# A two-layer encoder trunk: layer 0's first queries and keys as one 1024-output chunk, with the bias table and the last kept differences at other places

## The chip, the cores and the metric

The kernel runs on one core of a Trainium2 chip. The metric is the device time of one execution in microseconds (us). The engines are named as in the profile: PE is TensorE (matmuls; its weight loads are PEld), DVE is VectorE, ACT is ScalarE, POOL is GpSimd, SP is SyncE; the last three also issue DMAs.

## The reference

One sequence of 256 tokens, width 2048, passes two layers. Everything is float32.

```python
for i in range(DEPTH):                                  # 2 layers
    h = rms_norm(x, norm_attn[i])
    mkv = rms_norm(mem, norm_mem[i]) @ w_mem_kv[i]      # 256 memory tokens, 4 heads
    if i == 0:                                          # differential attention, 12 heads of 128
        q, k, v, q_m = split(h @ w_in_a, [1536, 3072, 4608])   # 5120 outputs
        q, k = rms_norm per 64 columns                  # two halves of a head
        o = (softmax(q1 k1 + bias) - lam * softmax(q2 k2 + bias)) v ; rms_norm ; * (1 - lam_init)
    else:                                               # windowed, 4 key heads, sink logit
        q, k, v, q_m = split(h @ w_in_b, [1536, 2048, 2560])
        o = softmax(q k + bias, sink) v                 # |distance| <= 128
    o_m = softmax(rms_norm(q_m) rms_norm(k_m)) v_m
    x = x + concat(o, o_m) @ w_out[i]
    x = x + square(relu(rms_norm(x, norm_mlp[i]) @ w_up[i])) @ w_down[i]   # 2048 -> 8192 -> 2048
```

The bias is one table of 32 distance buckets by 12 heads, looked up for every pair of positions.

## The kernel before, in words

**Products.** A float32 matrix is split into a high part (a cast on ACT, `split`, L450) and a low part (the difference, DVE, L451). A product of two such matrices is three matmuls: high by high, high by low, low by high (`three`, L541 to L544, or L503 to L505 in `chunk_tok`). A matmul has 128 rows of the inner dimension, 128 tokens and 512 outputs. Tokens stand as the stationary operand in two tiles t of 128.

**Weights.** All weights stream once from memory in pieces of 512 KB (128 x 1024 floats), issued on SP's queue (L395). `piece` hands out a piece whose split is done, and `fetch` keeps two more loaded and split ahead; the raw, high and low tiles are rings of four. The order of all pieces is the list `plan`.

**Seven products.** A pair is two pieces: 256 rows of the inner dimension by 1024 outputs, which with 256 tokens is a 2 x 2 by 2 x 2 block product. `seven` (L559) makes it with 7 block products, 21 matmuls, where `one_of_eight` needs 8, 24 matmuls. In exchange DVE and ACT make sums of weight blocks (`sum_pair`), differences of the token blocks (`differences`, `pair_differences`), and, once per group of outputs, sums of the side banks (`side_sums`, L578 to L581). Which pairs go so is set by tuples such as `KV_FAST` and `FAST`. `key_values` (L596) does layer 1's keys and values in this way: 8 pairs, of which 4 and 6 have seven products, four own banks (tag mm), four side banks (tag aux), and at the end own plus side (L631).

**Layer 0's input projection.** Ten chunks of 512 outputs by `chunk_tok`, 8 pieces and 96 matmuls each, in the order v0, q0, k0, v1, q1, k1, v2, q2, k2, qm (first values, first queries, first keys and so on; qm are the memory queries). During v0, `first` loads and splits x itself.

**Other work** runs between pieces. `tick` is called after each piece: it steps the light stages of all tasks that are due, and then up to `steps` heavy stages. A task has a wait and gaps, counted in ticks. Each engine then keeps the order in which its instructions were issued. Tasks that matter here:

- `prep`, the bias table: distances, then on DVE absolute values (L851), comparisons with thresholds (L852, L857), the side (L861), their sum (L863), and SP's DMA of the table to memory (L864). `PREP_AT` sets the tick, `scalars` makes lambda.
- `rows_done`, eight tasks: `bias_hot` reads 1/8 of the table back on POOL's queue (L887) and makes one-hots (L888); `bias_rows` looks the bias up with matmuls of 48 columns (L897). The heads wait for all eight.
- `norm_T`, the normalisation of queries and keys: squares on ACT (L646), their sums (L648, L649), inverse roots (L154 to L156), the product (L656, tile t2k), and the transposes on PE (L664).
- `diff_head`: the scores of a head, softmax, mix and output.

**The MLP.** The hidden state of each of 32 blocks j is made in the up projection; `keep` then makes its differences for the down projection's seven-product pairs and stores them in memory (`kept`, L1071, on ACT's queue), since the on-chip room is used by other things. The down loop runs twice (two halves of the outputs) over the 32 blocks, and `load_kept` reads a block's differences back on POOL's queue two blocks ahead. For the last four blocks `KEEP_LAST` says how many ticks after the hidden state their differences are made: for blocks 28 and 29 that falls in the down loop's first steps.

Of the kernel before, what the change touches and what calls it, by code (L numbers as in the profile page):

```python
# [32 lines left out]
BW = 14  # L33
# [3 lines left out]
KV_FAST = (4, 6)  # L37
DIFF_KV = {2: 4, 4: 6}
# [5 lines left out]
PREP_AT = 9  # L44
BGAP = 4
# [8 lines left out]
FAST = tuple(j for j in LATE if j not in (11, 20))  # L54
# [5 lines left out]
KEEP_LAST = (10, 18, 26, 34)  # L60
# [14 lines left out]
def trunk(ctx: ExitStack, tc: tile.TileContext, xin, xtok, memin, memtok, posrel, gcol, rows,  # L75
          w_a, w_b, w_kv, w_mem, w_out, w_up, w_down, out):
# [159 lines left out]
    weights = {"a": w_a, "b": w_b, "kv1": w_kv, "mem0": w_mem[0], "mem1": w_mem[1], "out0": w_out[0], "out1": w_out[1],  # L236
# [21 lines left out]
    for layer, (name, chunks) in enumerate((("a", (6, 0, 3, 7, 1, 4, 8, 2, 5, 9)), ("b", range(4)))):  # L258
        if layer:
            plan_pairs("kv1", 8, 1)  # L260
# [22 lines left out]
    def sums_tag(key):  # L283
        if key[0].startswith(("up", "kv")):
            return "h2"
# [40 lines left out]
    for i, (name, c, j) in enumerate(plan):  # L326
        at_piece.setdefault({"a": ("in", 0), "b": ("in", 1), "kv1": ("in", 1)}.get(name, (name[:-1], int(name[-1]) if name[-1].isdigit() else 0)), i)
# [27 lines left out]
    def sum_pair(name, c, p):  # L355
# [3 lines left out]
        up = name.startswith(("up", "kv"))  # L359
# [17 lines left out]
    def fetch(parts=1, lead=None):  # L377
# [18 lines left out]
        if name.startswith(("kv", "out", "up", "down")) and j % 2 == 0:  # L396
# [199 lines left out]
    def key_values(X2):  # L596
# [3 lines left out]
        for j in range(8):  # L600
            if j == KV_FAST[0]:
                side = [bank("aux") for _ in range(4)]
            if j in DIFF_KV:
                i = DIFF_KV[j]
# [7 lines left out]

            if j in KV_FAST:
                seven(own, side, j == KV_FAST[0], j == KV_FAST[-1], two, sums.pop(("kv1", 0, j)), at, diffs[j])
# [10 lines left out]
            if j == KV_FAST[-1]:  # L625
# [8 lines left out]
    def norm_T(ps, st, nseg, g, later=False):  # L634
# [35 lines left out]
        return (hi, lo), Task([Light(squares, 1), Light(rows, ROWS_GAP), tr][not later:], wait=WAIT if later else 1, gap=WAIT)  # L670
# [300 lines left out]
    def mem_ahead(j):  # L971
        if j == 5:
            load_mem(0)

    def mem_part(layer, qm, qd, H2):
        M2 = Halves()

        def before(j):
            if j % 2 == 0:
                if j:  # L980
                    mem_raw.pop(j // 2 - 1)
                if j < 6:
                    load_mem(j // 2 + 1)
            for k in (2 * j, 2 * j + 1):
                src = mem_raw[j // 2][:, k % 4, :]
                make_x2(M2, k, src, gc[:, G_MEM + layer * KT + k:G_MEM + layer * KT + k + 1])

# [64 lines left out]
    def mlp(layer, X2, last):  # L1052
# [9 lines left out]

        def keep(j, wait):
# [5 lines left out]
            def store():  # L1069
                kept[j] = dp.tile([P, 2, 512], F32R, name=nm("kept"))  # L1070
                nc.scalar.dma_start(as32(kept[j]), as32(box.pop()))  # L1071

            box = []
            Task([Light(make, KEEP_GAP), Light(store, 0)], wait=wait)
# [14 lines left out]
        def to_hidden(q, n, u, i, tag):  # L1089
# [14 lines left out]
            if any(j in fast_pairs(f"down{layer}", h) for h in range(2)):  # L1104
                keep(j, KEEP_AFTER[2 * n + i] if q < 7 else KEEP_LAST[2 * n + i])
# [46 lines left out]
        for half_ in range(2):  # L1152
# [30 lines left out]
            def load_kept(j):  # L1183
                if j in fast:
                    diff_in[j] = quad("h2", (P, 2, 512))
                    nc.gpsimd.dma_start(diff_in[j], kept[j])

            load_kept(1)
            for j in range(32):
# [6 lines left out]
                two.append(piece(f"down{layer}", half_, 2 * j + 1))  # L1196
                at = ats.popleft()
# [59 lines left out]
    rows_done = [Task([lambda i=i: bias_hot(i), lambda i=i: bias_rows(i, bias)], [prep], wait=BW, gap=BGAP) for i in range(8)]  # L1257
# [3 lines left out]
    loads = Task([lambda c=c: load_residual(c) for c in range(4)], wait=RES_AT, gap=RES_GAP, front=True)  # L1261
    for g in range(3):
# [23 lines left out]
    ps = chunk_tok("a", 9, X2, mem_ahead)  # L1286
# [20 lines left out]
    ps = chunk_tok("b", 3, X2, mem_ahead)  # L1307
# [74 lines left out]
```

## Time and profile before

| what | value |
|---|---|
| time, median of 3 runs | 2066.44 us (2066.3 to 2066.57) |
| the profiled execution's own time | 2068.06 us |
| its span, first to last instruction | 2066.3 us |
| PE, DVE, ACT busy | 2059.5, 1824.9, 1295.9 us |
| granted PE clock | 1.000 |
| v0 on PE ends, q0 begins | 28.7 us |
| kv chunk of layer 1 ends on PE | 1134.2 us |

The profile's times are from the start of the span. "PE mm L543 <- DVE lo L451: 1.3, 2, 0.8" reads: before matmuls of line 543 into a tile named mm, PE waited for the tile lo that DVE writes in line 451, 1.3 us in all, in 2 places, 0.8 us the longest. In a timeline, a row is a start, a duration, the engine, line and operation, out <- in with shapes, and in brackets the idle time before it with what ended it. Successive instructions of one engine overlap a little, so that the time that one takes from its engine is the distance of the starts.

### The profile page before, as it was taken

The page shows a single profiled execution, that of the slowest core. Times are in us where ns is not written, and L with a number is a line of the kernel's source. Part 1 is how long each engine was busy: PE and PEld are TensorE (multiplying, and loading weights), DVE is VectorE, ACT ScalarE, POOL GpSimd, SP SyncE. Part 2 cuts the span into 40 slices and gives each one's busy share as a digit, 9 for nine tenths or more (in the row PEclk, how much of TensorE's full clock was granted, in tenths as well). Part 3 has the DMA queues.
Part 4 walks back from the last instruction along what each step waited for, and adds up shares of the span by engine and source line. Part 5 has one row for each costly group of instructions (what it writes and reads, how often), then busy time and mean ns, then how long its engine had stood idle before and what let it go on. Part 6 is the DMA issues. An engine that isn't in the chain of part 4 may idle for free.

```text
span 2066.3 us, 28900 instructions
## 1 busy us (share of the span) xinstructions
PE 2059.5 (100%) x9966; PEld 1711.5 (83%) x9966; DVE 1824.9 (88%) x2659; ACT 1295.9 (63%) x1933; POOL 190.5 (9%) x292
## 2 busy tenths in 40 slices
PE   9999999999999999999999999999999999999999
PEld 7888888888888888888888888888888888888887
DVE  7677787898998999999999778889999999999998
ACT  7467665556566576767756556556566566676764
POOL 1200111100011100000002110000001111000000
PEclk9999999999999999999999999999999999999999
DMA  9678997877898998989978887577799999898994
GB/s 318 242 240 269 279 290 227 276 232 245 277 292 285 308 322 300 389 282 322 365 295 274 262 251 262 174 234 244 246 296 298 311 306 349 309 379 308 329 374 144
DMA packets 176099, 589.08 MB, mean 285 GB/s; under 512 B 20464, under 2 KB 21488, under 8 KB 174576
## 3 DMA queue, kind: packets, MB, share of 16 engines
q1 hardware_dynamic: 134128, 439.36, 59.5%
q0 software_dynamic: 36208, 127.94, 23.7%
q10 hardware_dynamic: 5616, 19.93, 2.4%
q8 instruction: 78, 1.28, 0.2%
q14 instruction: 69, 0.57, 0.1%
HBM read 552.42 MB, written 108.13 MB: 320 GB/s over the span
## 4 chain that ended last, share of the span: by engine, by line
PE 94%; DVE 3%; DMA 2%; issue 1%; ACT 1%; SPq 0%; DVEq 0%; ACTq 0%
PE mm L543 12%; PE mm L544 12%; PE mm L542 12%; PE aux L544 11%; PE aux L542 11%; PE aux L543 11%; PE mm L503 6%; PE mm L504 6%; PE mm L505 6%; DVE lo L451 1%; PE aux L687 1%; PE mm L1097 1%; PE aux L664 1%; PE aux L1097 1%; DMA kept<-h 1%
## 5 line engine op out<-in xcount | busy, mean ns | idle before, releaser
L451 DVE TENSOR_TENSOR lo<-raw,hi 128x1024 fp32r<-128x1024 f32 (+1 forms) x492 | 583.5, 1205 | 116.6 <-ACT hi L450 115.7
L450 ACT CAST hi<-raw 128x1024 fp32r<-128x1024 f32 (+1 forms) x492 | 495.6, 1035 | 287.8 <-PE mm L505 95.7
L503 PE MATMUL mm<-hi,x 128*128 128x512 f32 x576 | 231.5, 404 | 0.1
L504 PE MATMUL mm<-lo,x 128*128 128x512 f32 x576 | 225.6, 392 | 0.2 <-DVE lo L451 0.2
L505 PE MATMUL mm<-hi,x 128*128 128x512 f32 x576 | 225.2, 391 | 0.0
L450 ACT CAST h<-big 128x1024 fp32r<-128x1024 f32 (+1 forms) x100 | 100.4, 1021 | 131.7 <-DVE big L291 84.3
L542 PE MATMUL mm<-hi,x 128*128 128x512 f32 x464 | 181.3, 391 | 0.0
L543 PE MATMUL mm<-lo,x 128*128 128x512 f32 x464 | 180.7, 389 | 0.0
L544 PE MATMUL mm<-hi,x 128*128 128x512 f32 x464 | 180.6, 389 | 0.0
L543 PE MATMUL mm<-lo,h 128*128 128x512 f32 (+1 forms) x448 | 174.2, 389 | 1.3 <-DVE lo L451 1.3
L542 PE MATMUL mm<-hi,h 128*128 128x512 f32 (+1 forms) x448 | 174.1, 389 | 0.0
L544 PE MATMUL mm<-hi,h 128*128 128x512 f32 (+1 forms) x448 | 173.7, 388 | 0.0
L450 ACT CAST hi<-big 128x1024 fp32r<-128x1024 f32 (+1 forms) x138 | 120.8, 902 | 77.1 <-PE aux L544 35.9
L542 PE MATMUL aux<-hi,x 128*128 128x512 f32 x400 | 156.3, 391 | 0.0
L544 PE MATMUL aux<-hi,x 128*128 128x512 f32 x400 | 155.7, 389 | 0.0
L543 PE MATMUL aux<-lo,x 128*128 128x512 f32 x400 | 155.7, 389 | 0.0
L542 PE MATMUL aux<-hi,h 128*128 128x512 f32 x392 | 152.8, 390 | 0.0
L544 PE MATMUL aux<-hi,h 128*128 128x512 f32 x392 | 152.5, 389 | 0.0
L543 PE MATMUL aux<-lo,h 128*128 128x512 f32 x392 | 152.5, 389 | 0.0
L451 DVE TENSOR_TENSOR lo<-big,hi 128x1024 fp32r<-128x1024 f32 (+1 forms) x138 | 139.6, 1032 | 6.8 <-ACT hi L450 6.4
L451 DVE TENSOR_TENSOR h<-big,h 128x1024 fp32r<-128x1024 f32 (+1 forms) x100 | 116.8, 1179 | 30.8 <-ACT h L450 30.0
L505 PEld LDWEIGHTS mm<-hi,x 128*128 128x128 f32 x576 | 108.1, 188 | 23.8 <-DVE x L447 0.2
(318 smaller groups left out, 4452.5 us busy)
## 6 DMA issues: line engine op xcount, KB each, us to landing
raw<-in_w_up SPq DMA_DIRECT2D x164, 512.0 KB, 6.5
madesum<-in_w_down POOLq DMA_DIRECT2D x140, 512.0 KB, 6.6
raw<-in_w_down SPq DMA_DIRECT2D x112, 512.0 KB, 6.5
big<-in_w_up SPq DMA_DIRECT2D x92, 512.0 KB, 5.0
raw<-in_w_a SPq DMA_DIRECT2D x72, 512.0 KB, 5.3
h<-kept POOLq DMA_DIRECT2D x72, 512.0 KB, 6.9
raw<-in_w_out SPq DMA_DIRECT2D x52, 512.0 KB, 5.3
big<-in_w_down SPq DMA_DIRECT2D x46, 512.0 KB, 5.7
```

The lines of the kernel that those rows point to most:

```text
L450: nc.scalar.copy(hi, src)
L451: return nc.vector.tensor_tensor(lo, src, as32(hi), op=ALU.subtract)
L503: nc.tensor.matmul(ps[t], lhsT=xh, rhs=hi[:, ws], start=(k == 0), stop=False)
L504: nc.tensor.matmul(ps[t], lhsT=xh, rhs=lo[:, ws], start=False, stop=False)
L505: nc.tensor.matmul(ps[t], lhsT=xl, rhs=hi[:, ws], start=False, stop=(k == KT - 1))
L542: nc.tensor.matmul(acc_, lhsT=x(0), rhs=w2[0][:, ws], start=first_, stop=False)
L543: nc.tensor.matmul(acc_, lhsT=x(0), rhs=w2[1][:, ws], start=False, stop=False)
L544: nc.tensor.matmul(acc_, lhsT=x(1), rhs=w2[0][:, ws], start=False, stop=last_)
L664: nc.tensor.transpose(out=pt[:, h * P:(h + 1) * P], in_=qn[t][:, h * P:(h + 1) * P], identity=ident)
L687: nc.tensor.transpose(out=pt[:, kt * S + qt * P:kt * S + (qt + 1) * P], in_=p_of(qt)[:, kt * P:(kt + 1) * P], identity=ident)
L1097: nc.tensor.transpose(out=pt[:, oo * S + t * P:oo * S + (t + 1) * P], in_=u[n][t][:, o * P:(o + 1) * P], identity=ident)
```

## The change

1. q0 and k0 become one chunk of 1024 outputs, weights `w_qk` in pair layout, run by `two_chunks("qk0")`, which is `key_values` with a name; pairs 4 and 6 have seven products. `w_a` keeps the other eight chunks.
2. The bias table's tasks come later: `PREP_AT` 9 becomes 20, the hot rows' wait `BW` 14 becomes 22 and their gap 4 becomes 2, each of the eight tasks following the one three before it. `scalars` moves ahead. Two heavy steps for each tick are in v1 where they were in q0.
3. Blocks 28 and 29 of the hidden state no longer go through `keep`: in the first half of the down loop their differences are made in place two blocks ahead (`make_kept`), and stored then for the second half. Of the list of late blocks, 26 is left out of the seven-product pairs where 20 was.
4. The first memory rows are loaded one piece earlier, and the first pair of them is split in the chunk before; the layer-1 keys' norm has a rows gap of 2.

```diff
-BW = 14
+BW = 22
-KV_FAST = (4, 6)
-DIFF_KV = {2: 4, 4: 6}
+A_CHUNKS = (4, 5, 0, 2, 6, 1, 3, 7)
+TWO_FAST = (4, 6)
+DIFF_TWO = {2: 4, 4: 6}
-PREP_AT = 9
-BGAP = 4
+PREP_AT = 20
+BGAP = 2
-FAST = tuple(j for j in LATE if j not in (11, 20))
+FAST = tuple(j for j in LATE if j not in (11, 26))
-KEEP_LAST = (10, 18, 26, 34)
+KEEP_LATE = (28, 29)
...
+        if layer == 0:
+            plan_chunks(name, chunks[:1])
+            plan_pairs("qk0", 8, 1)
+            chunks = chunks[1:]
+        else:
             plan_pairs("kv1", 8, 1)
...
-    def key_values(X2):
+    def two_chunks(name, X2):
...
-            two = [piece("kv1", 0, 2 * j + i) for i in range(2)]
+            two = [piece(name, 0, 2 * j + i) for i in range(2)]
...
+        def store_kept(j, t2):
+            kept[j] = dp.tile([P, 2, 512], F32R, name=nm("kept"))
+            nc.scalar.dma_start(as32(kept[j]), as32(t2))
...
-                keep(j, KEEP_AFTER[2 * n + i] if q < 7 else KEEP_LAST[2 * n + i])
+                if j not in KEEP_LATE:
+                    keep(j, KEEP_AFTER[2 * n + i])
...
             def load_kept(j):
-                if j in fast:
+                if j in fast and (half_ or j not in KEEP_LATE):
                     diff_in[j] = quad("h2", (P, 2, 512))
                     nc.gpsimd.dma_start(diff_in[j], kept[j])
+
+            def make_kept(j):
+                if half_ == 0 and j in KEEP_LATE:
+                    diff_in[j] = quad("h2", (P, 2, 512))
+                    differences(diff_in[j], hids[j])
+                    Task([Light(lambda t2=diff_in[j]: store_kept(j, t2), 0)], wait=KEEP_GAP)
...
-    prep = Task([Light(load_rows, 0), Light(bias_distance, 0), Light(bias_float, PREP_AT - ROWS_AT)]
-                + [Light(f, 1) for f in (bias_size, scalars, lambda: bias_steps(12, 16), lambda: bias_steps(23, 32),
+    prep = Task([Light(load_rows, 0), Light(bias_distance, 0), Light(bias_float, 3), Light(scalars, PREP_AT - ROWS_AT - 3)]
+                + [Light(f, 1) for f in (bias_size, lambda: bias_steps(12, 16), lambda: bias_steps(23, 32),
...
-        ps = chunk_tok("a", 6 + g, X2, lead=first if g == 0 else None)
-        steps = 2 if g == 0 else 1
+        ps = chunk_tok("a", next(a_chunks), X2, lead=first if g == 0 else None, steps=2 if g == 1 else 1)
...
+            ps, ks = two_chunks("qk0", X2)
         else:
             val_f32(v, ps, st0)
-        ps = chunk_tok("a", g, X2, steps=steps)
+            ps = chunk_tok("a", next(a_chunks), X2)
         qT, qd = norm_T(ps, st0, 8, gs[:, 0:1])
-        ps = chunk_tok("a", 3 + g, X2)
-        kT, kd = norm_T(ps, st0, 8, gc[:, G_AK:G_AK + 1])
+        if g:
+            ks = chunk_tok("a", next(a_chunks), X2)
+        kT, kd = norm_T(ks, st0, 8, gc[:, G_AK:G_AK + 1])
...
-    kT, kd = norm_T(kv[0], st1, 4, gc[:, G_BK:G_BK + 1])
+    kT, kd = norm_T(kv[0], st1, 4, gc[:, G_BK:G_BK + 1], rows_gap=2)
```

In the changed kernel all lines stand some 5 (in the down loop some 20) further on: L451 is L456, L503 to L505 are L508 to L510, L543 is L548, L631 is L636, L648 and L649 are L653 and L654, L656 is L661, L664 is L669, L851 to L863 are L856 to L868, L1071 is L1084.

**How instructions move.** VectorE, around the bias table. In the kernel before, at the end of v0 and the start of q0 (lo are low parts of pieces, t2k_394, t2k_395 and t2k_310 the table's tiles):

```order
L451 TENSOR_TENSOR lo_314<-raw_312,hi_313 128x512
L852 TENSOR_SCALAR t2k_395<-t2k_394 128x512
L861 TENSOR_SCALAR t2k_310<-t2k_310 128x512
L857 SCALAR_TENSOR_TENSOR t2k_395<-t2k_394,t2k_395 128x512
L451 TENSOR_TENSOR lo_329<-raw_327,hi_328 128x1024
L857 SCALAR_TENSOR_TENSOR t2k_395<-t2k_394,t2k_395 128x512
L451 TENSOR_TENSOR lo_335<-raw_333,hi_334 128x1024
L857 SCALAR_TENSOR_TENSOR t2k_395<-t2k_394,t2k_395 128x512 x3
L451 TENSOR_TENSOR lo_359<-raw_357,hi_358 128x1024
L857 SCALAR_TENSOR_TENSOR t2k_395<-t2k_394,t2k_395 128x512 x2
```

In the changed kernel, from the first side sum (row 78 of VectorE's order) on; lo_713 and lo_719 are the low parts of v1's first two pieces, aux_573 to aux_575 side banks of the new stage, mm_355 to mm_358 its own banks:

```order
L583 TENSOR_TENSOR t2k_696<-aux_574,t2k_695 128x512
L456 TENSOR_TENSOR lo_713<-raw_711,hi_712 128x1024
L584 TENSOR_TENSOR t2k_698<-aux_573,t2k_696 128x512
L585 TENSOR_TENSOR t2k_697<-t2k_696,aux_575 128x512
L456 TENSOR_TENSOR lo_719<-raw_717,hi_718 128x1024
L586 TENSOR_TENSOR t2k_699<-t2k_697,aux_573 128x512
L856 SCALAR_TENSOR_TENSOR t2k_705<-t2k_310 128x512
L636 TENSOR_TENSOR t2k_695<-mm_355,t2k_695 128x512
L857 TENSOR_SCALAR t2k_706<-t2k_705 128x512
L636 TENSOR_TENSOR t2k_698<-mm_356,t2k_698 128x512
L862 SCALAR_TENSOR_TENSOR t2k_706<-t2k_705,t2k_706 128x512
L636 TENSOR_TENSOR t2k_697<-mm_357,t2k_697 128x512
```

and further on, up to v1's third piece (lo_782, row 102) and the table's end (L868):

```order
L862 SCALAR_TENSOR_TENSOR t2k_706<-t2k_705,t2k_706 128x512
L654 TENSOR_SCALAR sm_758<-sm_758,st_102 128x8
L862 SCALAR_TENSOR_TENSOR t2k_706<-t2k_705,t2k_706 128x512
L653 TENSOR_REDUCE sm_769<-t2k_770 128x8
L456 TENSOR_TENSOR lo_782<-raw_780,hi_781 128x1024
L654 TENSOR_SCALAR sm_769<-sm_769,st_102 128x8
L653 TENSOR_REDUCE sm_769<-t2k_774 128x8
L866 TENSOR_SCALAR t2k_310<-t2k_310 128x512
L654 TENSOR_SCALAR sm_769<-sm_769,st_102 128x8
L868 TENSOR_TENSOR t1k_799<-t2k_706,t2k_310 128x512
```

The table's operations, which stood one to three at a time between low parts at 25 to 36 us, now stand between the side sums, the own sums and the norm's sums, all of them ahead of lo_782 but the last two.

PE, at the first transposes of the queries. In the kernel before (tiles t2k_625 and t2k_627 are the normalised q0; hi_1083 and hi_1107 are v1's fourth and fifth pieces):

```order
L503 MATMUL mm_1045<-hi_1083,x_195 128x512
L504 MATMUL mm_1045<-lo_1084,x_195 128x512
L505 MATMUL mm_1045<-hi_1083,x_195 128x512
L664 MATMUL aux_1148<-ident,t2k_625 128x128 x4
L664 MATMUL aux_1155<-ident,t2k_627 128x128 x4
L503 MATMUL mm_1044<-hi_1107,x_223 128x512
```

In the changed kernel (hi_781 is v1's third piece, hi_827 its fourth; t2k_810 and t2k_812 the normalised q0):

```order
L508 MATMUL mm_779<-hi_781,x_168 128x512
L509 MATMUL mm_779<-lo_782,x_168 128x512
L510 MATMUL mm_779<-hi_781,x_168 128x512
L508 MATMUL mm_778<-hi_827,x_195 128x512
L509 MATMUL mm_778<-lo_828,x_195 128x512
L510 MATMUL mm_778<-hi_827,x_195 128x512
L508 MATMUL mm_779<-hi_827,x_195 128x512
L669 MATMUL aux_894<-ident,t2k_810 128x128 x4
L509 MATMUL mm_779<-lo_828,x_195 128x512
L669 MATMUL aux_901<-ident,t2k_812 128x128 x4
```

The transposes stood behind v1's fourth piece, with k0's whole chunk, and bias rows, between them and the end of q0. They stand now within v1's fourth piece, some 40 matmuls behind the end of the chunk that holds q0.

ACT, at the start of layer 0's down projection, before (h_8130 holds block 28's differences):

```order
L450 CAST h_8130<-t2k_8131 128x512
L450 CAST h_8155<-blk_5517 128x512
L450 CAST hi_8137<-big_4688 128x1024
L450 CAST hi_8160<-t2k_7999 128x512
L1071 DMA kept_8188<-h_8130 128x1024
L450 CAST h_8204<-blk_5891 128x512
L450 CAST x_8147<-blk_7818 128x1024
```

In the changed kernel, 100 rows later, in the 27th step of the loop:

```order
L455 CAST x_9158<-blk_7872 128x1024
L455 CAST h_9119<-t2k_9120 128x512
L1084 DMA kept_9150<-h_9119 128x1024
L455 CAST hi_9061<-raw_9060 128x1024
L455 CAST hi_9076<-raw_9075 128x1024
```

The store of block 28's differences, and the cast that makes them, moved from the first steps of the loop to its 27th.

More of the change, by code (lines that the diff above doesn't have):

```diff
@@ L256, in plan_pairs @@
         plan.extend((name, h, j) for h in range(halves) for j in range(2 * n))
-    for layer, (name, chunks) in enumerate((("a", (6, 0, 3, 7, 1, 4, 8, 2, 5, 9)), ("b", range(4)))):
-        if layer:
+    for layer, (name, chunks) in enumerate((("a", A_CHUNKS), ("b", range(4)))):
+        if layer == 0:
[3 more added lines that the diff above has]
+        else:
             plan_pairs("kv1", 8, 1)
@@ L283, in sums_tag @@
     def sums_tag(key):
-        if key[0].startswith(("up", "kv")):
+        if key[0].startswith(("up", "qk", "kv")):
             return "h2"
@@ L395, in fetch @@
             behind[0] = nc.sync.dma_start(raw, src)
-        if name.startswith(("kv", "out", "up", "down")) and j % 2 == 0:
+        if name.startswith(("qk", "kv", "out", "up", "down")) and j % 2 == 0:
             if down:
@@ L611, in at @@
                 return pair[:, kk, part, t * P:(t + 1) * P]
-            if j in KV_FAST:
-                seven(own, side, j == KV_FAST[0], j == KV_FAST[-1], two, sums.pop(("kv1", 0, j)), at, diffs[j])
+            if j in TWO_FAST:
+                seven(own, side, j == TWO_FAST[0], j == TWO_FAST[-1], two, sums.pop((name, 0, j)), at, diffs[j])
             elif j < 7:
@@ L632, in key_values, with norm_T @@
         return u
[L634 removed]
+    def norm_T(ps, st, nseg, g, later=False, rows_gap=ROWS_GAP):
         dim = 512 // nseg
@@ L669, in norm_T @@
             squares()
-        return (hi, lo), Task([Light(squares, 1), Light(rows, ROWS_GAP), tr][not later:], wait=WAIT if later else 1, gap=WAIT)
+        return (hi, lo), Task([Light(squares, 1), Light(rows, rows_gap), tr][not later:], wait=WAIT if later else 1, gap=WAIT)
     def val_f32(v, ps, st):
@@ L969, in load_mem, with memory, mem_ahead, ahead @@
         nc.sync.dma_start(mem_raw[i], memin[:, 1024 * i:1024 * i + 1024].rearrange("p (k s) -> p k s", s=S))
-    def mem_ahead(j):
-        if j == 5:
-            load_mem(0)
+    mem_x2 = {}
+    def memory(layer, j):
+        if j == 0:
+            mem_x2[layer] = Halves()
+        if j % 2 == 0:
+            if j:
+                mem_raw.pop(j // 2 - 1)
+            if j < 6:
+                load_mem(j // 2 + 1)
+        for k in (2 * j, 2 * j + 1):
+            src = mem_raw[j // 2][:, k % 4, :]
+            make_x2(mem_x2[layer], k, src, gc[:, G_MEM + layer * KT + k:G_MEM + layer * KT + k + 1])
+    def mem_ahead(layer):
+        def ahead(j):
+            if j == 4:
+                load_mem(0)
+            if j == 7:
+                memory(layer, 0)
+        return ahead
     def mem_part(layer, qm, qd, H2):
-        M2 = Halves()
+        M2 = mem_x2[layer]
         def before(j):
[L979 to L986, printed above, removed]
+            if j < 7:
+                memory(layer, j + 1)
         ps = chunk_tok(f"mem{layer}", 0, M2, before)
@@ L1067, in make @@
                 differences(box[0], hidden(j))
-            def store():
-                kept[j] = dp.tile([P, 2, 512], F32R, name=nm("kept"))
-                nc.scalar.dma_start(as32(kept[j]), as32(box.pop()))
             box = []
-            Task([Light(make, KEEP_GAP), Light(store, 0)], wait=wait)
+            Task([Light(make, KEEP_GAP), Light(lambda: store_kept(j, box.pop()), 0)], wait=wait)
         def h2_of(j):
@@ L1253, in trunk @@
     bias = big([P, 12, 2, S])
-    prep = Task([Light(load_rows, 0), Light(bias_distance, 0), Light(bias_float, PREP_AT - ROWS_AT)]
-                + [Light(f, 1) for f in (bias_size, scalars, lambda: bias_steps(12, 16), lambda: bias_steps(23, 32),
+    prep = Task([Light(load_rows, 0), Light(bias_distance, 0), Light(bias_float, 3), Light(scalars, PREP_AT - ROWS_AT - 3)]
+                + [Light(f, 1) for f in (bias_size, lambda: bias_steps(12, 16), lambda: bias_steps(23, 32),
                                          lambda: bias_steps(46, 64, 91), bias_side, bias_table)], wait=ROWS_AT, gap=1)
-    rows_done = [Task([lambda i=i: bias_hot(i), lambda i=i: bias_rows(i, bias)], [prep], wait=BW, gap=BGAP) for i in range(8)]
+    rows_done = []
+    for i in range(8):
+        rows_done.append(Task([lambda i=i: bias_hot(i), lambda i=i: bias_rows(i, bias)], [prep] + rows_done[max(0, i - 3):i - 2],
+                              wait=BW, gap=BGAP))
     Task([lambda: bias_save(bias)], rows_done)
```

35 lines of the change are left out of this document (19 added, 16 removed).

## The prediction

> **What bounds the kernel now.** I read the page first, then the waits of TensorE, then the windows around each place that the change touches.
>
> ```profile
> PE 2059.5 (100%) x9966; PEld 1711.5 (83%) x9966; DVE 1824.9 (88%) x2659; ACT 1295.9 (63%) x1933; POOL 190.5 (9%) x292
> ...
> PE 94%; DVE 3%; DMA 2%; issue 1%; ACT 1%; SPq 0%; DVEq 0%; ACTq 0%
> ```
>
> The first line is busy time by engine, the second the chain that ended last. TensorE runs without a break, so a matmul more or less is worth its issue interval, and a wait of TensorE is worth its length. VectorE at 88% is the next in line: it is off the path on average, and decides wherever much of its work stands ahead of a piece's low part.
>
> ```profile
> PE mm L543 <- DVE lo L451: 1.3, 2, 0.8
> PE aux L142 <- DVE ones L139: 1.1, 1, 1.1
> PE aux L664 <- DVE t2k L656: 0.7, 1, 0.7
> PE mm L504 <- DVE lo L451: 0.2, 1, 0.2
> PE aux L687 <- DVE t2k L805: 0.2, 1, 0.2
> ```
>
> These are the waits of TensorE (total, times, longest). So there is little to gain by removing waits: 1.5 us from the first and fourth rows, which the change touches, and 0.7 us in the third. Each ends on VectorE. Now the windows (length, then busy PE, PEld, DVE, ACT, POOL; then clock, DMA share and GB/s):
>
> ```profile
> 12.00:30.00 18.00, 18.00 (x77) 14.33 (x78) 17.77 (x43) 13.38 (x26) 1.67 (x3) 1.00 1.02 358
> 30.00:48.00 18.00, 18.00 (x81) 14.79 (x80) 14.97 (x24) 14.64 (x29) 2.81 (x6) 1.00 0.94 322
> 48.00:90.00 42.00, 42.00 (x397) 34.84 (x396) 29.08 (x43) 19.09 (x26) 14.80 (x27) 1.00 0.76 273
> 780.00:810.00 30.00, 29.18 (x130) 23.81 (x129) 28.59 (x35) 20.61 (x25) 1.59 (x3) 1.00 0.87 292
> ```
>
> The first 30 us have full DMA and a nearly full VectorE; from 48 to 90 us VectorE has 13 us to spare. At 780 to 810 us, the start of layer 0's down projection, it is full again.
>
> **The seven-product pairs.** Six matmuls of 512 columns go. Their interval, from the layer-1 twin of the new stage, where 24 of them lie between two rows:
>
> ```profile
> 1134.22 0.39 PE L503 MATMUL mm<-hi,x 128*128 128x512 f32 x1
> ...
> 1139.66 0.39 PE L503 MATMUL mm<-hi,x 128*128 128x512 f32 x1
> ```
>
> (1139.66 - 1134.22) / 24 = 0.2267 us; six are **-1.4**. The price is VectorE work at the stage's end. The twin shows it:
>
> ```profile
> 1130.48 0.68 DVE L578 TENSOR_TENSOR t2k<-aux,t2k 128x512 f32<-128x512 f32 x1
> ...
> 1134.79 0.67 DVE L648 TENSOR_REDUCE sm<-t2k 128x4 f32<-128x512 f32 x1
> 1135.39 0.68 DVE L631 TENSOR_TENSOR t2k<-mm,t2k 128x512 f32<-128x512 f32 x1
> 1135.98 0.22 DVE L649 TENSOR_SCALAR sm<-sm,st 128x4 f32<-128x4 f32 x1
> 1136.11 0.68 DVE L648 TENSOR_REDUCE sm<-t2k 128x4 f32<-128x512 f32 x1
> ...
> 1138.16 1.22 DVE L451 TENSOR_TENSOR lo<-raw,hi 128x1024 fp32r<-128x1024 f32 x1
> 1139.30 0.16 DVE L154 TENSOR_TENSOR sm<-sm 128x8 f32<-128x8 f32 x1
> ```
>
> Start to start, a 128x512 operation takes 0.60 us, L649 0.13 and a low part 1.14. There the first side sum starts 3.74 us before the next chunk's first matmul (1134.22), and that chunk's third piece has its low part at 1139.3. TensorE reaches it at the chunk's 26th matmul, 1139.9: in time by half a microsecond. So the twin has no room for more.
>
> In the changed order there is more. Between the first side sum and the low part of v1's third piece (rows 78 to 101) stand, on VectorE: nine operations of the bias table, four side sums, four of L636, three reductions (L653), two L654 and two low parts. The bias operations' price:
>
> ```profile
> 25.48 0.68 DVE L851 SCALAR_TENSOR_TENSOR t2k<-t2k 128x512 f32<-128x512 f32 x1
> 26.08 0.68 DVE L451 TENSOR_TENSOR lo<-raw,hi 128x512 fp32r<-128x512 f32 x1
> 26.69 0.41 DVE L852 TENSOR_SCALAR t2k<-t2k 128x512 f32<-128x512 f32 x1
> 27.02 0.41 DVE L861 TENSOR_SCALAR t2k<-t2k 128x512 f32<-128x512 f32 x1
> 27.36 0.68 DVE L857 SCALAR_TENSOR_TENSOR t2k<-t2k,t2k 128x512 f32<-128x512 f32 x1
> 27.96 1.21 DVE L451 TENSOR_TENSOR lo<-raw,hi 128x1024 fp32r<-128x1024 f32 x1
> ```
>
> That is 0.60 each for L851 and L857, 0.33 for L852. So 19 operations of 0.60, one of 0.33, two of 0.13 and two of 1.14: 14.3 us. Call E the end of the new stage on TensorE. The last side bank is finished 25 matmuls earlier (row 258 of 283); with 0.3 us to pass it on, the sums start at E - 5.4, and the third low part is done at E - 5.4 + 14.3 + 1.2 = E + 10.1. TensorE needs it after 26 matmuls, E + 5.9. **+4.2**, part of it already at v1's first matmul, whose bank L636 frees late. VectorE is then late for the next two things as well. Eleven matmuls on (2.5 us) comes the fourth piece's low part, with 1.9 us of other rows and 1.2 of its own ahead: **+0.6**. Three matmuls later TensorE meets q0's transposes, which want t2k_810: small operations 0.5, a low part 1.14 and the product 0.60 against 0.7 of matmuls: **+1.6**. In the kernel before, k0's whole chunk lay between q0's end and these transposes. Bounds of the three together: 0, if the cover of 51 matmuls from the side bank sufficed, to 8.
>
> Inside the new stage ACT has a raw piece's cast, which needs a free slot of the ring of four, ahead of the cast of the first pair's sum, so that sum's parts come about 0.5 late, and the second pair's 0.15: **+0.65** (bounds 0 and 2; by the ring's place in the order only, no row shows it).
>
> **The bias rows.** The table goes to memory and comes back before TensorE can use it:
>
> ```profile
> 35.51 0.69 DVE L863 TENSOR_TENSOR t1k<-t2k,t2k 128x512 bf16<-128x512 f32 x1
> 39.35 0.43 SPq L864 DMA_DIRECT2D bkt<-t1k  x1
> 45.19 4.88 POOL L887 DMA_DIRECT2D blk<-bkt  x9 [24.33 <-DMA bkt<-t1k]
> 53.99 0.75 DVE L888 TENSOR_SCALAR blk<-blk,itf 128x2048 bf16<-128x2048 bf16 x1
> 61.58 1.38 PE L897 MATMUL aux<-tab,blk 128*128 128x48 bf16 x48
> ```
>
> From the store's issue to the first one-hot's end are 54.74 - 39.35 = 15.4 us, and TensorE came 6.8 later. In the change the table ends near E + 12 (five rows after that third low part), the one-hot at E + 27.4 by the same span, or E + 24.4 if the two transfers land in two thirds of their time, as VectorE and DMA are emptier there. TensorE is at that place, 36 rows past the transposes, at E + 24.1. **+1.4**, bounds 0.3 and 3.3. The bias rows end a chunk later, and three heads' scores then come together on four banks: **+0.4** (0 to 1.2; before, the heads' work shows only the 0.2 at L687). What moves out of 25 to 36 us frees the first chunk's change: the 0.2 at L504 goes, **-0.2**.
>
> **The kept differences.** At the down projection's start ACT's queue stands behind the store of a difference:
>
> ```profile
> 792.84 6.17 DMA kept<-h
> ...
> 799.02 0.62 ACT L450 CAST h<-blk 128x512 fp32r<-128x512 f32 x1 [2.79 <-DMA kept<-h]
> ...
> 800.63 1.22 DVE L451 TENSOR_TENSOR x<-big,x 128x1024 fp32r<-128x1024 f32 x1 [1.41 <-ACT x L450]
> ...
> 804.78 0.39 PE L542 MATMUL mm<-hi,h 128*128 128x512 f32 x1
> 805.99 0.50 PE L543 MATMUL mm<-lo,h 128*128 128x512 f32 x1 [0.82 <-DVE lo L451]
> ...
> 1767.53 5.86 DMA kept<-h
> ...
> 1780.37 0.50 PE L543 MATMUL mm<-lo,h 128*128 128x512 f32 x1 [0.50 <-DVE lo L451]
> ```
>
> A cast waits for that store's end to reuse its buffer, VectorE idles 1.41 us for the cast, TensorE is late by 1.21 - 0.23 = 0.98 us, and 0.66 in layer 1 (0.50 and the same 0.16 of restart). With these two differences moved to the loop's 27th and 28th steps the store isn't there: **-1.6** (bounds 0, if VectorE's full window makes its own lateness, and -1.9). At the new place their VectorE work, about 1.4 us each, lies in a stretch with room:
>
> ```profile
> 810.00:1085.00 275.00, 275.00 (x1222) 227.71 (x1221) 264.49 (x317) 186.63 (x239) 16.37 (x31) 1.00 0.91 329
> ```
>
> 10.5 us idle of 275, TensorE never waiting: 0, and up to +1 each if all fell in one step. The four loads that go from POOL's queue are covered by the same stretch.
>
> **The rest.** VectorE's and TensorE's orders in layer 1's key norm are the same with a rows gap of 2, so its 0.7 us stays. The memory load and first memory pair a little earlier lie in a stretch without waits: 0.
>
> **Sum**: -1.4 - 0.2 - 1.6 + 4.2 + 0.6 + 1.6 + 0.65 + 1.4 + 0.4 = +5.65. The profiled execution took 2068.06 us with a span of 2066.3; the three runs' median is 2066.44. The difference is applied to that: 2072.1, I say **2072.0**.
>
> **Rivals.** About 0.2% (4.1 us: under 2062.3 or over 2070.6) is what a measurement can tell from no change.
>
> *The sums find cover.* Everything at v1 is one race: the block of VectorE work against 51 matmuls (11.6 us). From under 10.1 us of block, instead of 14.3, TensorE waits for none of the three, and the gains stand alone: 2066.44 - 3.2 = 2063.2 with the rest at 0. For it: VectorE idles 13 us of the 42 around. Against: that idle time lies elsewhere, as the block starts with a bank that TensorE finishes late. Only with layer 1's 0.7 gone as well, and some, does it pass 2062.3. Chance 0.17, of which 0.05 below 2062.3.
>
> *Half of it.* The sums, the fourth piece and the transposes overlap more than I add (3 us in all) and the one-hot comes in time: 2066.4 to 2068. For it: each later wait is counted from the previous one's end. Chance 0.17.
>
> *A slower clock after the pause.* All windows above have clock 1.00, with no wait over 1.1 us. Here TensorE would pause 3 to 4 us in one go. If the clock then halved, the 14 matmuls up to the transposes would cost 14 x 0.227 = 3.2 us more, of which 0.6 + 1.6 are waits for VectorE anyway: +1.0, or the full 3.2 if it comes where nothing waits: 2073 to 2075. [...] Chance 0.10.
>
> *Transfers late.* The new stage loads two pairs ahead, while the windows before 48 us already show 0.94 to 1.02 of DMA. A 512 KB piece at 358 GB/s is 1.5 us; two pieces out of turn give +3: 2075. Against: the kernel before ran these windows without a wait. Chance 0.08.
>
> My forecast has the remaining 0.48. Slower by over 0.2%: 0.45 of it, the clock and the transfers, 0.63; same: 0.32; faster: 0.05. The range: 2063.5 to 2076 leaves about a tenth at either end; the forecast's own is 2070 to 2074.5.
>
> **What would show it.** In the changed profile, waits of TensorE at L509 or L508 on L456 or L636 between 70 and 85 us, some 5 us in all, and at L669 on L661 about 1.6. Right at the down projections: no store of a kept difference there, no wait at L548. Wrong: no wait over 1 us in the first 90 us; or waits on DMA there, which would be the fourth rival; or a clock below 1.00 behind the pause.

## The result and the profile after

The changed kernel takes 2079.15 us (median of 4 runs, 2078.08 to 2083.84) against 2066.37 us: a ratio of 1.0059, 95% interval 1.0047 to 1.0071, 12.8 us slower. Slower was forecast as likeliest, but 2072.0 us with a range up to 2076: the sign was right and the size was less than half of it. The profiled execution took 2079.69 us with a span of 2077.9, 11.6 over the span before.

The page of the changed kernel, busy time and the chain that ended last:

```profile
PE 2062.0 (99%) x9960; PEld 1711.8 (82%) x9960; DVE 1839.1 (89%) x2687; ACT 1299.4 (63%) x1940; POOL 189.9 (9%) x288
...
PE 88%; DVE 6%; DMA 3%; ACT 1%; issue 1%; SPq 0%; ACTq 0%; DVEq 0%
```

Six matmuls are gone, and VectorE's share of the chain has doubled. TensorE's waits (total, times, longest):

```profile
PE mm L509 <- DVE lo L456: 3.5, 2, 3.3
PE aux L669 <- DVE t2k L661: 2.2, 4, 1.2
PE aux L711 <- ACT blk L451: 1.7, 1, 1.7
PE aux L143 <- DVE ones L140: 1.1, 1, 1.1
PE aux L902 <- DVE blk L893: 1.0, 1, 1.0
PE mm L548 <- DVE lo L456: 0.7, 2, 0.5
PE mm L508 <- DVE t2k L636: 0.6, 1, 0.6
PE mm L508 <- ACT hi L455: 0.5, 1, 0.5
...
PE aux L711 <- DVE sm L717: 0.4, 1, 0.4
```

The first, fifth and seventh rows are v1 and the first bias rows, as forecast. The second is only in small part the transposes of q0: most of it lies at 290 us (1.2) and in layer 1 (0.7, as before). The third and the last are scores of heads, which were forecast at 0.4 us in all.

VectorE's timeline at the end of the new stage: the first side sum, the first operation of the bias table, the first of L636, and the low part of v1's third piece.

```profile
67.02 0.68 DVE L583 TENSOR_TENSOR t2k<-aux,t2k 128x512 f32<-128x512 f32 x1
...
71.68 0.69 DVE L856 SCALAR_TENSOR_TENSOR t2k<-t2k 128x512 f32<-128x512 f32 x1
72.28 0.69 DVE L636 TENSOR_TENSOR t2k<-mm,t2k 128x512 f32<-128x512 f32 x1
...
81.27 1.22 DVE L456 TENSOR_TENSOR lo<-raw,hi 128x1024 fp32r<-128x1024 f32 x1
```

The block is 81.27 - 67.02 = 14.25 us long; the prediction had 14.3. TensorE behind it, and the windows (busy PE, PEld, DVE, ACT, POOL, then clock, DMA share, GB/s) of its pause and of the time after:

```profile
82.54 0.79 PE L509 MATMUL mm<-lo,x 128*128 128x512 f32 x1 [3.29 <-DVE lo L456]
83.13 0.63 PE L510 MATMUL mm<-hi,x 128*128 128x512 f32 x1
83.56 0.63 PE L509 MATMUL mm<-lo,x 128*128 128x512 f32 x1
```

```profile
78.80:82.50 3.70, 0.46 (x3) 0.03 (x1) 3.70 (x8) 2.42 (x5) 0.00 (x0) 0.99 0.00 0
82.50:86.00 3.50, 3.46 (x9) 2.73 (x10) 3.50 (x11) 0.43 (x2) 0.00 (x0) 0.53 0.61 181
```

After the pause the granted clock is 0.53 and matmuls come 0.43 us apart instead of 0.227: the third rival's slow clock is there.

**Where the 11.6 us lie.** Against the interval that each kind of matmul has when nothing waits, I summed what every interval had too much, in both traces, by stretch. After minus before:

| stretch of the program | us |
|---|---|
| start and v0 | +0.2 |
| q0 and k0, v1 up to the first bias rows (28 to 100 us) | +7.8 |
| the rest of layer 0's attention (100 to 310 us) | +5.5 |
| six matmuls fewer | -1.4 |
| start of layer 0's down projection | -1.0 |
| start of layer 1's down projection | -0.8 |
| end of layer 0's down projection and layer 1's keys and values | +0.7 |
| end of layer 1's down projection | +0.5 |
| remaining stretches together | +0.1 |

The prediction's terms for the second row are 0.65 + 4.2 + 0.6 + 1.6 + 1.4 - 0.2 = 8.25. So the block at v1 was sized right. The third row had 0.4.

VectorE in that stretch, windows of the kernel before and then of the changed kernel:

```profile
100.00:141.00 41.00, 41.00 (x262) 32.96 (x261) 29.55 (x89) 25.35 (x55) 1.62 (x2) 1.00 0.65 233
...
200.00:260.00 60.00, 60.00 (x312) 49.67 (x312) 44.07 (x101) 36.88 (x81) 7.73 (x10) 1.00 0.91 279
```

```profile
100.00:141.00 41.00, 41.00 (x459) 34.04 (x458) 23.93 (x28) 18.35 (x23) 10.93 (x18) 1.00 0.69 231
...
200.00:260.00 60.00, 60.00 (x318) 49.57 (x317) 46.89 (x123) 38.09 (x92) 7.23 (x9) 1.00 0.82 244
```

From 100 to 141 us VectorE does 5.6 us less work than before, and ACT 7.0 less, because no head has begun (the first scores are at 141.72 us; before, at 112.25). That work comes later, into stretches where pieces and norms need the same engines. Of the third row some 4 us lie between 141 and 200 us and 3 between 200 and 310; up to 141 us the changed kernel loses about 1 us less than the kernel before, whose first heads are there.

### The profile page after: what moved, and what is told of

Its sections match the earlier page's. It is cut to its first block, busy times and chain, and to the rows that moved or that the text cites. A ratio compares the mean times of both kernels' runs of the same rounds, so it can differ in the third digit from the quotient of the medians.

```text
span 2077.9 us, 28913 instructions
## 1 busy us (share of the span) xinstructions
PE 2062.0 (99%) x9960; PEld 1711.8 (82%) x9960; DVE 1839.1 (89%) x2687; ACT 1299.4 (63%) x1940; POOL 189.9 (9%) x288
## 4 chain that ended last, share of the span: by engine, by line
PE 88%; DVE 6%; DMA 3%; ACT 1%; issue 1%; SPq 0%; ACTq 0%; DVEq 0%
PE mm L548 12%; PE mm L549 12%; PE mm L547 12%; PE aux L549 11%; PE aux L548 11%; PE aux L547 11%; PE mm L508 4%; PE mm L510 4%; PE mm L509 4%; DVE lo L456 2%; DMA raw<-in_w_kv 1%; PE aux L1116 1%; PE mm L1116 1%; DMA raw<-in_w_a 1%; PE aux L692 1%
## 5 line engine op out<-in xcount | busy, mean ns | idle before, releaser
L456 DVE TENSOR_TENSOR lo<-raw,hi 128x1024 fp32r<-128x1024 f32 (+1 forms) x488 | 578.6, 1206 | 124.7 <-ACT hi L455 123.7
L455 ACT CAST hi<-raw 128x1024 fp32r<-128x1024 f32 (+1 forms) x488 | 490.6, 1035 | 285.6 <-PE mm L510 81.0
L508 PE MATMUL mm<-hi,x 128*128 128x512 f32 x512 | 205.8, 403 | 1.2 <-DVE t2k L636 0.6
L510 PE MATMUL mm<-hi,x 128*128 128x512 f32 x512 | 201.5, 394 | 0.0
L548 PE MATMUL mm<-lo,x 128*128 128x512 f32 x514 | 200.6, 390 | 0.5 <-DVE lo L456 0.5
L549 PE MATMUL mm<-hi,x 128*128 128x512 f32 x514 | 200.3, 390 | 0.0
L547 PE MATMUL mm<-hi,x 128*128 128x512 f32 x514 | 199.4, 391 | 0.4 <-ACT hi L455 0.4
L548 PE MATMUL mm<-lo,h 128*128 128x512 f32 (+1 forms) x450 | 174.7, 388 | 0.2 <-DVE lo L456 0.2
L548 PE MATMUL aux<-lo,x 128*128 128x512 f32 x402 | 156.5, 389 | 0.0
L548 PE MATMUL aux<-lo,h 128*128 128x512 f32 x392 | 152.6, 389 | 0.0
L456 DVE TENSOR_TENSOR lo<-big,hi 128x1024 fp32r<-128x1024 f32 (+1 forms) x140 | 142.3, 1037 | 3.6 <-ACT hi L455 3.3
L456 DVE TENSOR_TENSOR h<-big,h 128x1024 fp32r<-128x1024 f32 (+1 forms) x100 | 116.9, 1180 | 30.1 <-ACT h L455 29.3
L509 PEld LDWEIGHTS mm<-lo,x 128*128 128x128 f32 x512 | 97.0, 189 | 22.4 <-DVE lo L456 5.1
```

The costliest lines, as they stand in the source:

```text
L455: nc.scalar.copy(hi, src)
L456: return nc.vector.tensor_tensor(lo, src, as32(hi), op=ALU.subtract)
L508: nc.tensor.matmul(ps[t], lhsT=xh, rhs=hi[:, ws], start=(k == 0), stop=False)
L509: nc.tensor.matmul(ps[t], lhsT=xh, rhs=lo[:, ws], start=False, stop=False)
L510: nc.tensor.matmul(ps[t], lhsT=xl, rhs=hi[:, ws], start=False, stop=(k == KT - 1))
L547: nc.tensor.matmul(acc_, lhsT=x(0), rhs=w2[0][:, ws], start=first_, stop=False)
```

## The experiments

The theory was that one cause, the bias table's operations put into the busy end of the new stage, makes both large rows: directly at v1, and through late heads afterwards. The rivals: the seven-product sums alone are too much; the slow clock; the other parts of the change. Times are medians; ratios are against the kernel before, run on the same chip in the same set. Its median was 2068.29 in the first set, 2067.45 and 2067.4 in the others.

### The table at its old tick

```diff
-PREP_AT = 20
+PREP_AT = 9
```

> The changed kernel with the bias table's operations back at tick 9 (PREP_AT 9 in place of 20), all else as changed. My theory: the nine bias operations (5.2 us of VectorE) between the first side sum and the low part of v1's third piece are what makes TensorE wait. Without them the block is 9.1 us instead of 14.3, and TensorE's 51 matmuls (11.6 us) cover it: the wait of 3.45 us there, the 0.8 at v1's first matmul, the 1.1 before the first bias rows and the slow clock behind the pause go, 6 to 8 us in all: 2071 to 2073. Rival: the side sums and the norm alone are too much, the wait shrinks to 1 to 2 us and stays, 2075 to 2077.

2067.96 us, ratio 1.0001 (0.9991 to 1.001). Its waits:

```profile
PE mm L548 <- DVE lo L456: 1.6, 3, 0.8
...
PE aux L711 <- DVE sm L717: 0.6, 1, 0.6
PE aux L669 <- DVE t2k L661: 0.4, 1, 0.4
PE mm L509 <- DVE lo L456: 0.2, 1, 0.2
```

With this one number the 12 us are gone, 4 to 6 more than expected. No wait is left at v1's third piece, none at the first bias rows, and from 100 to 310 us TensorE loses less than 1 us more than in the kernel before, so the heads' loss came from the table's place as well. In exchange the new stage now waits in its first half (0.8 and 0.5 us at 37 and 42 us), which makes up for the six matmuls and the kept differences.

The wait at v1 went, but not because the block shrank as expected. VectorE's first side sum and the low part of v1's third piece, then TensorE's first matmul with that low part:

```profile
68.50 0.68 DVE L583 TENSOR_TENSOR t2k<-aux,t2k 128x512 f32<-128x512 f32 x1
...
80.94 1.22 DVE L456 TENSOR_TENSOR lo<-raw,hi 128x1024 fp32r<-128x1024 f32 x1
```

```profile
82.22 0.50 PE L509 MATMUL mm<-lo,x 128*128 128x512 f32 x1
```

The block is 80.94 - 68.50 = 12.4 us long, not 9.1: the table's nine operations left it, but two one-hots (L893), two copies of looked-up bias (L903) and some more of the norm came into it. In return TensorE looks up two of the eight groups of bias rows ahead of the third piece, at 73.88 and 77.48 us, which lengthens the cover by 1.2 us each. The low part is ready at 82.16 us, just in time for 82.22. So the run shows what the table's place is worth; whether the side sums and the norm alone would fit under 51 matmuls, the rival's question, it doesn't show.

### Late heads by themselves

The kernel before, where nothing but the bias rows' start is moved:

```diff
-BW = 14
+BW = 24
```

> The kernel before with nothing changed but the bias rows ten ticks later (BW 24 instead of 14), so that the first heads' scores stand 96 matmuls (22 us) later, about where the changed kernel has them; its table, its chunks and VectorE's work around v1 are as before. Theory: late heads cost by themselves, since their VectorE and ACT work is crowded into fewer chunks; waits at scores and at the transposes of later queries appear as in the changed kernel: 3 to 4.6 us more than before. Rival: the cost of the heads in the changed kernel came from three of them in one go and the backlog that v1's wait left; here 0 to 1 us.

2073.31 us, ratio 1.0024 (1.0016 to 1.0033): 3.3 to 6.8 us slower, without any other part of the change. The profiled execution is the fastest of its eleven; its waits, and the two windows from above:

```profile
PE aux L664 <- DVE sm L714: 1.8, 1, 1.8
...
PE aux L664 <- DVE t2k L656: 0.9, 2, 0.6
PE mm L543 <- DVE lo L451: 0.8, 1, 0.8
PE mm L503 <- ACT hi L450: 0.6, 1, 0.6
PE aux L706 <- ACT x L446: 0.3, 1, 0.3
```

```profile
100.00:141.00 41.00, 41.00 (x368) 33.56 (x368) 25.87 (x53) 21.18 (x37) 1.62 (x2) 1.00 0.69 242
...
200.00:260.00 60.00, 59.73 (x326) 48.85 (x323) 46.50 (x126) 38.59 (x93) 7.24 (x9) 1.00 0.81 243
```

As in the changed kernel, VectorE has less to do up to 141 us, more after 200, and TensorE waits for transposes of a later chunk. So late heads cost by themselves, and about as much as the changed kernel loses in its third row. The places are the same only in part. Here the first scores are at 133.82 us, 21.6 us later than before, and one head follows another by 3.9 us; in this profile TensorE loses 4.7 us more than before from 200 to 310 us, and nothing more from 141 to 200. The changed kernel lost 3 us in the former stretch and 4 in the latter, with heads 29 us late and three heads' scores within 4 us. Whether those 4 us come from the greater lateness, from the three heads in one go or from the backlog behind v1 was not tried apart; the run with the table at its old tick shows that they go with the table's place.

### The pause and the clock

> The changed kernel with 14 matmuls (3.2 us) of no use put ahead of v1's third piece, where TensorE pauses 3.45 us; their result is not read. Theory: the pause makes the half clock behind it (seven intervals of 0.427 instead of 0.227), so here the clock stays 1.00 and the intervals 0.227; but VectorE sets the time of the next low part and of the transposes, so TensorE waits there instead, and the total stays within 0.5 us of the changed kernel: 2078.7 to 2079.6. Rival: the half clock costs by itself, 7 times 0.2: 2077.7.

```diff
+            if w == "a" and c == A_CHUNKS[1] and j == 2:
+                spare = bank()
+                for _ in range(FILL):
+                    nc.tensor.matmul(spare, lhsT=X2[0][:, 0, 0:P], rhs=hi[:, 0:512], start=True, stop=True)
             hi, lo = piece(w, c, j, lead and (lambda i: lead(2 * j + i)))
```

With FILL = 14: 2077.26 us, ratio 1.0047 (1.0032 to 1.0062). Five of the matmuls went into the 0.8 us wait at v1's first matmul, nine ahead of the third piece, where the wait is 1.0 us; the clock stays at 1.00. It is 1.9 us under the changed kernel's median (2.5 by the ratios, since the two were run in different sets), as the rival said, but the two intervals overlap. So this run doesn't decide what the slow clock costs.

> The changed kernel with 4 matmuls of no use ahead of v1's third piece instead of 14: the pause becomes some 2.5 us instead of 3.45 or 0.3 to 1.1. [...]

With FILL = 4: 2079.44 us, ratio 1.006 (1.0045 to 1.0075). All four went into the wait at v1's first matmul, so that the pause kept its length (3.4 us over the usual interval), and the first matmul behind it took 0.79 us as in the changed kernel, against 0.50 with FILL = 14. The pause of 2.5 us that was wanted, to see whether the clock stays at 1.00 behind it, didn't come about there, but further on the same trace has one of 2.0 us:

```profile
290.76 1.12 PE L674 MATMUL aux<-ident,t2k 128*128 128x128 f32 x4 [2.02 <-DVE t2k L666]
```

The granted clock is 0.50 from 290.73 us on, and these four transposes took 1.12 us, against 0.63 in the changed kernel at 87.70 us, where it is 1.00. So this pause of 2.0 us had half the clock behind it too; the last section comes back to this.

What the clock costs can be read from a pair of versions that were run for another reason (the next two). Both pause 3.25 us for the same low part; in one the clock falls, in the other not. First the version without the memory part, rows of TensorE and windows:

```profile
83.05 0.79 PE L509 MATMUL mm<-lo,x 128*128 128x512 f32 x1 [3.25 <-DVE lo L456]
...
88.98 0.60 PE L669 MATMUL aux<-ident,t2k 128*128 128x128 f32 x4
```

```profile
79.40:83.00 3.60, 0.40 (x2) 0.00 (x0) 3.60 (x7) 2.40 (x5) 0.00 (x0) 0.85 0.00 0
83.00:88.40 5.40, 5.35 (x13) 4.20 (x14) 5.40 (x13) 1.11 (x3) 1.04 (x2) 0.50 0.61 183
```

Then the version with the memory rows' squares three ticks after their loads:

```profile
84.27 0.50 PE L509 MATMUL mm<-lo,x 128*128 128x512 f32 x1 [3.25 <-DVE lo L456]
...
89.42 0.63 PE L669 MATMUL aux<-ident,t2k 128*128 128x128 f32 x4 [1.18 <-DVE t2k L661]
```

```profile
80.60:84.20 3.60, 0.42 (x2) 0.00 (x0) 3.60 (x7) 2.42 (x5) 0.00 (x0) 1.00 0.00 0
84.20:88.00 3.80, 3.50 (x14) 2.47 (x14) 3.80 (x12) 0.63 (x3) 0.00 (x0) 1.00 0.50 172
```

From the end of the pause to q0's transposes it is 5.93 us at half clock and 5.15 at the full one: 0.8 us. The slow clock added some 2.6 us to 13 intervals, and most of it took the place of waits for VectorE (1.18 at the transposes and 0.2 before), as the prediction's third rival had it with +1.0. It isn't what made the 12.8 us.

### The memory part, and the memory rows' squares

```diff
-            if j == 4:
-                load_mem(0)
-            if j == 7:
-                memory(layer, 0)
+            if j == 5:
+                load_mem(0)
...
-            if j < 7:
-                memory(layer, j + 1)
+            memory(layer, j)
...
-    kT, kd = norm_T(kv[0], st1, 4, gc[:, G_BK:G_BK + 1], rows_gap=2)
+    kT, kd = norm_T(kv[0], st1, 4, gc[:, G_BK:G_BK + 1])
```

> The changed kernel without its fourth part: memory rows loaded at piece 5 and their first pair split in the memory chunk as before, rows gap of 1. Theory: the first memory pair's split (0.47 us each on VectorE, plus casts) ahead of the memory queries' norm makes the 1.3 us wait at 289.6 us; without it that wait goes: 2077.8. Rival: that wait comes from the heads that are late by then, and stays: 2079.1.

2079.02 us, ratio 1.0053 (1.0036 to 1.0069): the wait at 290 us stays, and is 1.6 us in its profile. The fourth part of the change costs and brings nothing that can be seen here.

```diff
-            parts.append(Task([Light(lambda i=i, box=box: load(i, box), 0), Light(lambda i=i, box=box: square(i, box), MEM_GAP)],
+            parts.append(Task([Light(lambda i=i, box=box: load(i, box), 3), Light(lambda i=i, box=box: square(i, box), MEM_GAP)],
```

> The changed kernel with each load of memory rows three ticks ahead of its square on ACT, instead of right before it. Theory: the 1.7 us wait of the scores at 189.5 us comes from ACT standing behind a transfer of memory rows; it goes, and the time is 1.5 to 1.8 us under the changed kernel. Rival: the heads are late anyway, another wait takes its place: under 0.5 us.

2079.23 us, ratio 1.0059 (1.0044 to 1.0074). The scores' wait on ACT at 189.5 us did go, and the time didn't: the wait at 290 us grew from 1.2 to 2.8 us, and the one at the first bias rows was 2.0 instead of 1.0 in this profile, which is of the slowest of the four executions. With the heads late, taking away this wait moved the loss to other places.

### The kept differences alone

The kernel before with `make_kept`, `KEEP_LATE` and pair 26 left out in place of 20:

```diff
-FAST = tuple(j for j in LATE if j not in (11, 20))
+FAST = tuple(j for j in LATE if j not in (11, 26))
-KEEP_LAST = (10, 18, 26, 34)
+KEEP_LATE = (28, 29)
...
+                make_kept(j + 2)
```

> The kernel before with the third part of the change alone: blocks 28 and 29 of the hidden state get their differences in the down loop, pair 26 without seven products instead of 20. My theory: the two waits at the starts of the down projections (0.98 and 0.66 us) go and nothing takes their place: 2066.4 - 1.6 to 1.9, 2064.5 to 2064.8. Rival: VectorE is full there, or the changed profile's new wait of 0.33 us near 1882 us and its 0.7 us in layer 1 belong to this part: 2065.5 to 2066.4.

2066.65 us, ratio 0.9995 (0.9985 to 1.0004).

> The third part of the change alone on the kernel before, the same kernel as in the first set of runs, for a narrower interval: 1.6 us under the kernel before, ratio 0.9992. Rival: none of it is left: 1.0000.

2066.39 us, ratio 0.9996 (0.9987 to 1.0005). Both waits at the starts of the down projections are gone, in these two and in the changed kernel, whose window there shows TensorE without a gap:

```profile
780.00:830.00 50.00, 50.00 (x228) 41.58 (x227) 47.54 (x55) 39.33 (x52) 3.76 (x7) 1.00 0.95 341
```

By the traces that is worth 1.8 us, by the times 1.0 and 0.8 us with an interval that holds zero. The difference isn't settled: some of these profiles have 0.3 to 0.6 us of new waits in layer 1's keys and values, at places that change from one execution to the next.

### Looking for a better place

The table at tick 12, into VectorE's idle time between 28 and 48 us:

```diff
-PREP_AT = 20
+PREP_AT = 12
```

> The changed kernel with the bias table at tick 12 instead of 20. VectorE is idle for 7.9 of 20 us between 28 and 48 us in the changed kernel, and full from 48 to 83 us. Theory: the table's 5.8 us fit into that idle stretch; no wait in v1 as with tick 9, and the two waits that tick 9 has at 36 and 41 us (0.96 and 0.7) shrink: 0.5 to 1.3 us less than with tick 9, just under the kernel before. Rival: those waits come from the transfers (DMA share 1.0 there), and stay: the same time as with tick 9.

2068.8 us, ratio 1.0005 (0.9995 to 1.0015). The waits before 50 us are 1.1 and 1.3 us, no smaller than with tick 9: the rival held. Then also the token rows later:

```diff
-RES_AT = 8
+RES_AT = 13
-SQ_WAIT = 3
+SQ_WAIT = 7
```

> Tick 12 for the bias table, and the four loads of the token rows for the row statistics (2 MB) five ticks later (RES_AT 13, their squares at SQ_WAIT 7), into the stretch where the changed kernel's DMA share is 0.2 to 0.4. Theory: the share of 1.0 between 28 and 48 us is why the new stage's pieces come late there; without the 2 MB the waits before 50 us go (1.0 to 2 us together in the other versions): 0.5 to 1.5 us less than with tick 12 alone. Rival: the pairs' own 2 MB fill the queue, no difference; or the statistics come late for the norm: slower.

2067.19 us, ratio 0.9999 (0.9989 to 1.0008). TensorE's losses between 28 and 50 us fall from 3.8 to 1.5 us in the two profiles, and the median by 1.6, though the two intervals overlap; so by the traces the token rows' loads and their squares on ACT were most of it; which of the two was not tried apart. Its scores still came two heads at a time, hence the last version, which has the bias rows earlier and one heavy step for each tick:

```diff
-BW = 22
+BW = 20
...
-        ps = chunk_tok("a", next(a_chunks), X2, lead=first if g == 0 else None, steps=2 if g == 1 else 1)
+        ps = chunk_tok("a", next(a_chunks), X2, lead=first if g == 0 else None, steps=1)
```

> The changed kernel with the table at tick 12, the token rows' loads at tick 13 and their squares after them, and the bias rows two ticks earlier (BW 20) with one heavy step for each tick in v1 instead of two, so that no two heads' scores stand together. Theory: of the 1.5 us that the version with tick 12 and late token rows loses against the kernel before, some 1 us is at those scores; with the kept differences' 1.6 and the six matmuls' 1.4 it ends 1 to 3 us under the kernel before. Rival: the bias rows now want side banks that VectorE frees late, TensorE waits there, no gain.

2067.54 us, ratio 0.9999 (0.999 to 1.0008). Its waits:

```profile
PE mm L548 <- DVE lo L456: 1.2, 3, 0.6
PE aux L143 <- DVE ones L140: 1.1, 1, 1.1
PE aux L669 <- DVE t2k L661: 0.6, 1, 0.6
```

The scores' wait is gone, but the 1 to 3 us were not gained: the time is that of the kernel before. What is left are waits inside the new stage and at layer 1's norm. Even well placed, the new stage gives back about what its six matmuls save: with it the median is 1.1 us above that of the kept differences alone, in the same set. No version here beats the kernel before by more than its interval.

## Why the prediction was right or wrong

**The block at v1: right in its size.** The block's length was 14.25 us for 14.3, its start 5.3 us before the stage's end for 5.4. The wait that it makes, with v1's late first matmul, was 0.80 + 3.45 = 4.25 us for 4.2; the next low part, the transposes and the slow clock together 2.3 for 2.2. That the sum came out so well is partly luck in its last piece: 0.6 and 1.6 were forecast as two waits at full clock, and most of it came as half clock, with only 0.18 us of waiting at the transposes.

**The new stage's own waits: right in size.** Forecast +0.65, measured +0.6 (ending at 29.9, 41.1 and 47.5 us); but the places are in its first half, and not where ACT's order had put them. The version with the token rows later, on another placing of the table, took 2.3 us from such waits.

**The first bias rows: right.** +1.4 forecast; 1.0 us of waiting.

**The heads: the step that failed.** The sentence "The bias rows end a chunk later, and three heads' scores then come together on four banks: +0.4" costed the scores' own place in TensorE's order, and took everything behind them as unchanged. At that place it was sized well: the waits among the first scores are 0.1 and 0.35 us. But the late heads measured +5.5 from 100 to 310 us. The heads' VectorE and ACT work moved by 29 us, out of a stretch with room and into stretches shared with pieces, norms of later queries and memory rows, and its lateness shows up there as waits at transposes, at scores of the next group and at a cast behind a transfer. The late bias rows alone, in the kernel before, cost 3.3 to 6.8 us, in the profile from 200 us on; which part of lateness makes the changed kernel's 4 us between 141 and 200 us stays open. The bound of 1.2 that the prediction gave stood beside the waits of a kernel in which no head was late (0.2 at L687), and so bounded nothing.

**The gains: right.** Six matmuls -1.4. The kept differences -1.6 forecast, -1.0 and -0.8 in the trace.

**The start of the stage: wrong, by 0.2.** The 0.2 us at L504 at the start of q0 went with the table, but at 29.9 us, nearly the same place, there is now a wait of 0.4.

**Not foreseen, +1.2:** waits near the end of the down projections and in layer 1's keys and values. Other versions, also the one with the kept differences alone, show 0.3 to 1.4 us there in changing places. What makes them was not tried.

**The rivals.** That the sums find cover didn't come, and the point of 10.1 us from which it was to decide was not tested: with the table at its old tick no wait is left at v1, but the block there is 12.4 us and two groups of bias rows lengthen the cover. The slow clock was given a chance of 0.10 and was seen; that it would be one half was my assumption, as the windows of the kernel before all have 1.00. It was 0.53 in the 3.5 us behind the changed kernel's pause and 1.00 from 86 to 90 us, and 0.50 for 5.4 us in the version without the memory part. Its net cost, 0.8 us between two other versions, is near the 1.0 that was worked out, and as a rival it asked for that much more, not for 7. The range, up to 2076, was too narrow because none of the rivals had late work as its mechanism.

## What to carry to other kernels

When a task is moved later, cost not only the place where it lands but all the work that waits for it: how much engine time that work needs, and whether the stretches into which it is now squeezed have that time free. A list of waits of a kernel in which nothing is late puts no upper bound on what lateness costs. And once an engine has a backlog, removing one wait moves it to the next: remove what made the backlog.

## What the runs showed of the hardware

In these runs the length of the pause alone didn't decide the granted clock behind it. Pauses with the same 3.25 us of waiting led to 0.50 in the version without the memory part (83.00 to 88.40 us) and to 1.00 in the one with the memory rows' squares later (84.20 to 88.00 us). The changed kernel's pause of 3.29 us led to 0.53 (82.50 to 86.00 us), and the one of 2.02 us with FILL = 4 to 0.50. The version that kept its clock at 84 us lost it at a shorter pause, of 2.83 us, 200 us later; the rows there, and the windows of the pause and of the time after:

```profile
293.30 0.66 PE L669 MATMUL aux<-ident,t2k 128*128 128x128 f32 x4 [2.83 <-DVE t2k L661]
...
295.71 0.63 PE L509 MATMUL mm<-lo,x 128*128 128x512 f32 x1
296.13 0.63 PE L510 MATMUL mm<-hi,x 128*128 128x512 f32 x1
```

```profile
290.00:293.00 3.00, 0.47 (x3) 0.05 (x1) 2.93 (x9) 0.96 (x2) 0.00 (x0) 1.00 0.96 227
293.00:297.00 4.00, 3.70 (x19) 3.39 (x20) 4.00 (x8) 2.43 (x5) 0.51 (x1) 0.69 1.05 315
```

The clock is 0.69 in the mean of these 4 us, and the last two matmuls come 0.42 us apart, against 0.43 behind the changed kernel's pause. What made the difference between the two pauses of 3.25 us was not shown.
